# Loading the two norms' scale and offset rows through GpSimd's queue, and making the scaled residual during the down projection

## The chip, the cores and the metric

The kernel runs on one core of one Trainium2 chip. The metric is the device time of one execution in microseconds. The five engines of the core run their own instruction streams and meet at semaphores: TensorE (PE in the rows; PEld is its weight load), VectorE (DVE), ScalarE (ACT), GpSimd (POOL) and SyncE (SP). Transfers are issued by an engine's queue (SPq, ACTq, POOLq in the rows) and carried by 16 DMA engines.

## The reference

One encoder layer on 256 tokens of width 2048. What matters here is its second half: a layer norm, a gated feed-forward of width 5632, a residual, and a second layer norm.

```python
mixed = concat(rms_norm(attn), rms_norm(ssm)) @ w_out
x = layer_norm(ALPHA * x + mixed, ln1_g, ln1_b)          # norm 1
up = x @ w_ffn_in                                         # 2048 -> 2 * 5632
gate = causal_depthwise_conv(up[..., :D_FF], conv_w, conv_b)
hidden = gelu(gate) * up[..., D_FF:]
ff = hidden @ w_ffn_out                                   # 5632 -> 2048
x = layer_norm(ALPHA * x + ff, ln2_g, ln2_b)             # norm 2
```

`ln1_g`, `ln1_b`, `ln2_g` and `ln2_b` are rows of 2048 numbers. The kernel keeps them as four rows of a tensor `rows` in device memory.

## The kernel before

**The stream of weights.** All products take their weights from one stream of chunks of 128x1024 float32 (512 KB). `run` (L176) walks over them. In turn j it splits chunk j+3, issues the load of chunk j+7 on SP's queue, and then writes chunk j's matmuls. A load goes into one of four buffers `raw` (`dma_chunk`, L145). The split (`split_chunk`, L151) makes the high part `hi` on ScalarE (L163) and the rest `lo` on VectorE (L164), each into one of four buffers. So a load waits until VectorE has done with the `raw` buffer four chunks earlier, and a split waits until TensorE has done with the `hi` and `lo` buffers four chunks earlier. SP issues in order: a load behind a waiting one waits too.

**The order.** The code is written out in one order, in which small jobs (`side`) put in a piece after a given chunk; a scheduler then places the instructions on the engines, and each engine runs its own list in order.

**Around norm 1.** The last products of `w_out` (tile `os`) end in `evac_os` (L1112), which adds them onto `res`, the tile [128, 2, 2048] that holds the residual of both token tiles. `ln1` (L1138) normalizes one token tile without scale and offset in place in `res` (L1148; one quarter on ScalarE, L1146), transposes it on TensorE (L1153, tile `lt`), applies scale and offset per partition on ScalarE (L1156, tile `lnt`), and VectorE splits it into the stationary-side activations `x1s` (L1160 and L1161). Norm 1's second token tile runs while TensorE does the first feed-forward product for the first token tile alone (L226).

**Feed-forward.** 44 blocks of four chunks (weights `wf`, tile `f`, `mm_f`, L214) fill the hidden tiles `hid`. Then come 88 chunks of the down projection (weights `wd`, tile `d`, `mm_b`, L237): four column blocks of 22 chunks, each with two PSUM banks, in turns of banks 0, 1 and 2, 3. At a column block's end `evac_down` (L1305) does `res = ALPHA * res + d` on VectorE. `x1s` lies in the buffer tagged `xs`; it is free when the last feed-forward product (chunk 175) has been done.

**The residual.** `res` has to hold norm 1 with its scale and offset before the first `evac_down`. `residual` (L1245) does this in eight pieces of 256 columns: it loads the scale and the offset piece, each broadcast over the partitions, into small tiles `rg` and `rb` (two buffers each) on SP's queue, and GpSimd multiplies and adds them onto both token tiles (L1257, L1258). `load_gb2` (L1266) loads norm 2's two full rows on SP's queue into the buffer `xs`, early in the down projection.

Of the kernel before, what the change touches and what calls it, by code (L numbers as in the profile page):

```python
# [12 lines left out]
F32 = mybir.dt.float32  # L13
# [3 lines left out]
ALU = mybir.AluOpType  # L17
PSUM = bass.MemoryType.PSUM
DRAM = bass.MemoryType.DRAM

P = 128
SEQ = 256
DM = 2048
# [8 lines left out]
NP_ = G // 2  # L32
# [25 lines left out]
def host_layout(x, w_in, attn_rel_bias, ssm_a_re, ssm_a_im, ssm_log_dt, ssm_b_re, ssm_b_im,  # L58
                ssm_c_re, ssm_c_im, ssm_d, w_glu, b_glu, g_attn_out, g_ssm_out, w_out,
                ln1_g, ln1_b, w_ffn_in, ffn_conv_w, ffn_conv_b, w_ffn_out, ln2_g, ln2_b):  # L60
    a = {}
    xs = x[0]
# [21 lines left out]

    # groups by (half, column): pairs as they are, and the order whose transposes are pairs
    col, half = np.arange(NP_)[None, :], np.arange(2)[:, None]
# [32 lines left out]
class Builder:  # L119
# [6 lines left out]

# [1 line left out]
    def fill(self):  # L128
# [8 lines left out]

# [1 line left out]
    def add(self, src, mm, post=None, hold=None):  # L139
# [58 lines left out]

# [1 line left out]
    def mm_a(self, ps, hi, lo, xs, k0, first, last, nk=8):  # L200
# [13 lines left out]
    def mm_f(self, ps, hi, lo, k0, first, last, part=None):  # L214
        """product with x1, whose columns are (token tile, high or low part, token)"""
        nc, xs = self.nc, self.x1
        th = lambda a: a.rearrange("p (t h c) -> p t h c", t=2, h=2)[:, :, 0]
        for kk in range(8):
            x = xs[:, k0 + kk]
            w = slice(kk * P, (kk + 1) * P)  # L220
            start, stop = first and kk == 0, last and kk == 7

            def low():
                nc.tensor.matmul(th(ps), lhsT=lo[:, w], rhs=th(x), start=False, stop=False)  # L224
            if part == 0:
                nc.tensor.matmul(ps[:, 0:SEQ], lhsT=hi[:, w], rhs=x[:, 0:SEQ], start=start, stop=False)  # L226
                continue
            c = slice(0, 512) if part is None else slice(SEQ, 512)
            if stop:
                low()  # L230
            nc.tensor.matmul(ps[:, c], lhsT=hi[:, w], rhs=x[:, c], start=start and part is None, stop=stop)  # L231
            if not stop:
                low()
# [23 lines left out]

# [1 line left out]
    def build(self):  # L259
# [30 lines left out]

    # phase 1 -----------------------------------------------------------------
    def plan_phase1(self):
# [83 lines left out]
        add_v(1)  # L376
        # k, q
        for j in range(8):
            for c in range(4):
# [9 lines left out]
                self.add(I["wkq"][4 * j + c], mm, post)  # L389
        # w_out, attention half  # L390
        def wo_attn(nb, c):
# [8 lines left out]
        for nb in (2, 3):  # L400
            for c in range(4):
                wo_attn(nb, c)
        # glu
        for f in range(8):
# [3 lines left out]
            self.add(I["wg"][f], mm, lambda f=f: self.evac_glu(f, cur["ps"]))  # L408
        # w_out, state half; the last two blocks one token tile after the other
        for nb in range(4):  # L410
# [53 lines left out]
    def evac_ab(self, ps, name, scale=None):  # L464
        """second half of a product of the split operands, copied out of PSUM"""
        t = self.t1([P, SEQ], name)
        if scale is None:
            self.nc.scalar.copy(t, ps[:, SEQ:])
        else:
            self.nc.scalar.mul(t, ps[:, SEQ:], scale)  # L470
        return t
# [34 lines left out]

    # S5 ----------------------------------------------------------------------
    def s5_load(self):
# [40 lines left out]
    def s5_params(self):  # L549
# [46 lines left out]
        exp(dec, dec)  # L596
        # sin and cos by the quadrant of th
        ts(k, th, 0.6366197723675814, MUL, MAGIC, ADD)
# [62 lines left out]
        def cmul(o, ia, a, b, w):  # L661
            # o, a: [P, 2, 4, NP_] tiles at index; (o = a*b)
            (orr, oi), (ar, ai), (br, bi) = o, a, b
# [11 lines left out]
        ts(self.scb[:, 1], self.scb[:, 1], -1.0, MUL)  # L675
        # a^(s) f B, s = 0..3
        MB = self.MB = bp.tile([P, 2, NP_, 4, SG], F32, tag="d0", name="MB")
# [29 lines left out]
        ops.append((0.2, lambda: V.tensor_copy(cB[:, 1], PA[:, 1, 3])))  # L707
        # -C_im
        ts(self.sc[:, 1], self.sc[:, 1], -1.0, MUL)
# [3 lines left out]
    def reorder(self, a, o):  # L713
        """values of the groups in the order of the transposes, brought to the order of the pairs"""
        nc = self.nc
# [112 lines left out]
    def s5_kstack(self):  # L828
# [39 lines left out]
        for g2 in range(2):  # L868
            for i in range(4):
                # rows s >= 3-i hold the kernel of lag s-(3-i)  # L870
                n = SG * (i + 1)
# [5 lines left out]
    def s5_cm(self):  # L877
# [8 lines left out]
        for pg in range(4):  # L886
# [20 lines left out]
            for ri in range(2):  # L907
                # C holds (re, -im): re(C a) and -im(C a)
                Gp.tensor_tensor(t0, cr if ri == 0 else ci, ar, op=ALU.mult)
# [42 lines left out]
    def evac_glu(self, f, ps):  # L952
# [7 lines left out]
        nc.vector.tensor_tensor(s, ps[:, 0:SEQ], t, op=ALU.add)  # L960
        # sigmoid(z) = (1 + tanh(z / 2)) / 2; the half is taken at the group's norm
        nc.scalar.activation(s, s, AF.Tanh, bias=self.bh[:, f:f + 1], scale=0.5)
# [35 lines left out]

    # attention -----------------------------------------------------------------
    def attention(self, j):  # L1000
# [85 lines left out]

    # w_out and layer norm 1 ------------------------------------------------------
    def load_x(self):
# [81 lines left out]

    # phase 2 -----------------------------------------------------------------
    def plan_phase2(self):
# [37 lines left out]
        for nb in range(4):  # L1210
            for c in range(22):
# [29 lines left out]
                self.add(I["wd"][22 * nb + c], mm, post if c == 21 else None, hold)  # L1241
        self.side(12, self.residual())
        self.side(178, self.load_gb2())

    def residual(self):  # L1245
        nc, fp = self.nc, self.fp
        for q in range(8):
            c = slice(q * 256, (q + 1) * 256)
            g = fp.tile([P, 256], F32, tag="rg", name=f"rg{q}")
            b = fp.tile([P, 256], F32, tag="rb", name=f"rb{q}")  # L1250
            nc.sync.dma_start(g, self.I["rows"][0, c].partition_broadcast(P))
            nc.sync.dma_start(b, self.I["rows"][1, c].partition_broadcast(P))
            yield
            yield
            for tt in range(2):
                r = self.res[:, tt, c]
                nc.gpsimd.tensor_tensor(r, r, g, op=ALU.mult)  # L1257
                nc.gpsimd.tensor_tensor(r, r, b, op=ALU.add)  # L1258
            yield

# [4 lines left out]

    def load_gb2(self):  # L1266
        nc = self.nc
        t = self.bp.tile([P, 2, DM], F32, tag="xs", name="gb2")
        self.g2, self.b2 = t[:, 0], t[:, 1]
        nc.sync.dma_start(self.g2, self.I["rows"][2].partition_broadcast(P))  # L1270
        nc.sync.dma_start(self.b2, self.I["rows"][3].partition_broadcast(P))
        self.st2 = [self.cp.tile([P, n, 6], F32, name=f"st2{n}") for n in (4, 8)]
        yield
# [75 lines left out]
```

## Time and profile before

| | before |
|---|---|
| median of 3 runs | 1163.69 us (1162.95 to 1164.85) |
| span of the profiled execution, first to last instruction | 1161.2 us |
| median of the runs less that span | 2.5 us |
| TensorE busy | 1120.5 us, 96% of the span |
| VectorE / ScalarE / GpSimd busy | 67% / 48% / 10% |
| mean granted TensorE clock | 0.985 |

The profile is of one execution. Its spans, waits and clocks are read in microseconds from the first instruction. [...]

### The profile page before, as it was taken

Reading aid. Unit: us, or ns where it says so; the run is one execution under the profiler, and the core shown is the slowest. Engines: PE = TensorE matmul, PEld = TensorE weight load, DVE = VectorE, ACT = ScalarE, POOL = GpSimd, SP = SyncE. Lnnn points to the kernel's source line nnn. Section 1 sums busy time; section 2 is a strip of 40 time slices with the busy share of each in tenths; the row PEclk is TensorE's granted clock in tenths of the full one; section 3 lists DMA queues with packets and bytes.
Section 4 is the critical chain, followed back from the end, with each engine's and each line's share of the span. In section 5 each row is a group of like instructions: output and inputs, shape, how many; then the busy total and the mean of one; then the engine's idle time right before and its main releaser. Section 6 shows DMA issues by size and latency. Waiting matters only on the chain.

```text
span 1161.2 us, 18034 instructions
## 1 busy us (share of the span) xinstructions
PE 1120.5 (96%) x6936; PEld 946.9 (82%) x6936; DVE 772.8 (67%) x1379; ACT 563.1 (48%) x849; POOL 121.6 (10%) x125
## 2 busy tenths in 40 slices
PE   8999959999999889999999999999999999999996
PEld 6887747887787778888888888888888888888885
DVE  7993399994678866666666666666666545454555
ACT  5454325553666545555555555555555433333350
POOL 2031870000001270000000000000000000000001
PEclk9999979999999989999999999999999999999998
DMA  8786324443666446556656666666665766666661
GB/s 299 281 234 147 104 83 146 155 150 97 225 193 204 150 140 212 183 182 189 190 184 183 194 185 182 185 187 190 185 186 190 258 196 192 193 196 192 190 198 73
DMA packets 63589, 212.04 MB, mean 183 GB/s; under 512 B 7568, under 2 KB 13072, under 8 KB 62864
## 3 DMA queue, kind: packets, MB, share of 16 engines
q1 hardware_dynamic: 62320, 208.38, 57.7%
q0 software_dynamic: 896, 2.10, 0.8%
q8 instruction: 54, 0.88, 0.3%
q10 hardware_dynamic: 288, 0.43, 0.1%
q14 instruction: 31, 0.25, 0.1%
HBM read 207.46 MB, written 3.41 MB: 182 GB/s over the span
## 4 chain that ended last, share of the span: by engine, by line
PE 88%; DVE 7%; DMA 2%; POOL 1%; issue 1%; ACT 1%; SPq 0%; ACTq 0%; POOLq 0%; DVEq 0%
PE f L231 27%; PE f L224 14%; PE d L247 7%; PE d L249 7%; PE d L245 7%; PE kq L209 3%; PE u L209 2%; DVE lo L164 2%; PE kq L211 2%; PE oa L245 1%; PE oa L247 1%; PE u L211 1%; PE oa L249 1%; PE glu L209 1%; PE v L247 1%; PE v L249 1%
## 5 line engine op out<-in xcount | busy, mean ns | idle before, releaser
L164 DVE TENSOR_TENSOR lo<-raw,hi 128x1024 fp32r<-128x1024 f32 (+1 forms) x358 | 441.0, 1233 | 246.0 <-ACT hi L163 242.2
L163 ACT CAST hi<-raw 128x1024 fp32r<-128x1024 f32 (+1 forms) x358 | 374.4, 1046 | 299.8 <-PE d L249 125.9
L231 PE MATMUL f<-x1s,hi 128*128 128x512 f32 (+1 forms) x1408 | 491.2, 398 | 6.4 <-ACT hi L163 4.2
L224 PE MATMUL f<-x1s,lo 128*128 128x256 f32 x1408 | 382.6, 283 | 0.5 <-DVE lo L164 0.5
L231 PEld LDWEIGHTS f<-x1s,hi 128*128 128x128 f32 x1408 | 261.2, 190 | 63.1 <-ACT hi L163 4.5
L224 PEld LDWEIGHTS f<-x1s,lo 128*128 128x128 f32 x1408 | 268.0, 190 | 9.5 <-DVE lo L164 1.0
L247 PE MATMUL d<-lo,hid 128*128 128x512 f32 (+1 forms) x360 | 133.4, 371 | 0.0
L245 PE MATMUL d<-hi,hid 128*128 128x512 f32 (+1 forms) x360 | 133.4, 370 | 0.0
L249 PE MATMUL d<-hi,hid 128*128 128x512 f32 (+1 forms) x360 | 133.3, 370 | 0.0
L209 PE MATMUL kq<-xs,hi 128*128 128x512 f32 x240 | 89.8, 412 | 3.1 <-DVE qt L505 3.1
L1324 POOL TENSOR_TENSOR res<-res,gb 128x416 f32<-128x416 f32 x2 | 2.9, 1444 | 721.6 <-ACT res L1323 721.6
L245 PEld LDWEIGHTS d<-hi,hid 128*128 128x128 f32 x360 | 67.8, 188 | 11.8
L247 PEld LDWEIGHTS d<-lo,hid 128*128 128x128 f32 x360 | 67.8, 188 | 11.6
L249 PEld LDWEIGHTS d<-hi,hid 128*128 128x128 f32 x360 | 67.8, 188 | 11.5
L211 PE MATMUL kq<-xs,lo 128*128 128x256 f32 x240 | 69.2, 288 | 0.0
L209 PEld LDWEIGHTS kq<-xs,hi 128*128 128x128 f32 x240 | 45.6, 190 | 14.5 <-DVE qt L505 3.5
L1279 ACT COPY ga<-f 128x256 f32<-128x256 f32 x44 | 16.4, 374 | 82.4 <-PE f L231 82.4
L1286 DVE TENSOR_TENSOR gp<-f,ga 128x256 f32<-128x256 f32 x44 | 18.7, 425 | 45.0 <-ACT ga L1279 45.0
L1279 ACT COPY va<-f 128x256 f32<-128x256 f32 x44 | 16.3, 371 | 64.7 <-PE f L231 64.7
L1298 DVE TENSOR_TENSOR va<-f,va 128x256 f32<-128x256 f32 x44 | 18.7, 424 | 42.3 <-ACT va L1279 42.3
L211 PEld LDWEIGHTS kq<-xs,lo 128*128 128x128 f32 x240 | 45.8, 191 | 0.9
L209 PE MATMUL u<-xs,hi 128*128 128x512 f32 x120 | 43.5, 401 | 0.0
(214 smaller groups left out, 1418.1 us busy)
## 6 DMA issues: line engine op xcount, KB each, us to landing
raw<-wf SPq DMA_DIRECT2D x176, 512.0 KB, 3.7
raw<-wd SPq DMA_DIRECT2D x88, 512.0 KB, 4.3
raw<-wkq SPq DMA_DIRECT2D x32, 512.0 KB, 3.6
raw<-wo SPq DMA_DIRECT2D x32, 512.0 KB, 3.9
raw<-wu SPq DMA_DIRECT2D x16, 512.0 KB, 4.5
raw<-wv SPq DMA_DIRECT2D x15, 512.0 KB, 6.1
raw<-wg SPq DMA_DIRECT2D x8, 512.0 KB, 4.4
bd<-band SPq DMA_DIRECT2D x16, 128.0 KB, 3.0
```

The source lines that it names most:

```text
L163: self.nc.scalar.copy(hi[:, c], raw[:, c])
L164: self.nc.vector.tensor_tensor(lo[:, c], raw[:, c], hi[:, c].bitcast(F32), op=ALU.subtract)
L209: nc.tensor.matmul(ps, start=first and kk == 0, stop=False, **h)
L211: nc.tensor.matmul(ps[:, 0:SEQ], start=False, stop=False, **l)
L224: nc.tensor.matmul(th(ps), lhsT=lo[:, w], rhs=th(x), start=False, stop=False)
L231: nc.tensor.matmul(ps[:, c], lhsT=hi[:, w], rhs=x[:, c], start=start and part is None, stop=stop)
L245: nc.tensor.matmul(ps, lhsT=ah, rhs=wh, start=first and kk == 0, stop=False)
L247: nc.tensor.matmul(ps, lhsT=ah, rhs=wl, start=False, stop=False)
L249: nc.tensor.matmul(ps, lhsT=al, rhs=wh, start=False, stop=last and kk == 1)
L1279: self.nc.scalar.copy(tv, v[:, :, 1])
L1286: nc.vector.tensor_tensor(g[:, 2:].rearrange("p (t c) -> p t c", t=2), p0, t, op=ALU.add)
L1298: nc.vector.tensor_tensor(tv, p0, tv, op=ALU.add)
```

## The change

`residual` and `load_gb2` are gone. In their place one job `load_gb` is put in after chunk 176, the first chunk of the down projection. It loads all four rows in full, each 2048 columns broadcast over 128 partitions (1 MB written each), by GpSimd's queue into one tile of the buffer `xs`. Behind them on GpSimd stand the multiplications and additions of the residual, now in four column blocks of 512. Norm 2 reads its rows from the same tile. The rest of the difference is comments.

```diff
-        self.side(12, self.residual())
-        self.side(178, self.load_gb2())
-
-    def residual(self):
-        nc, fp = self.nc, self.fp
-        for q in range(8):
-            c = slice(q * 256, (q + 1) * 256)
-            g = fp.tile([P, 256], F32, tag="rg", name=f"rg{q}")
-            b = fp.tile([P, 256], F32, tag="rb", name=f"rb{q}")
-            nc.sync.dma_start(g, self.I["rows"][0, c].partition_broadcast(P))
-            nc.sync.dma_start(b, self.I["rows"][1, c].partition_broadcast(P))
-            yield
-            yield
-            for tt in range(2):
-                r = self.res[:, tt, c]
-                nc.gpsimd.tensor_tensor(r, r, g, op=ALU.mult)
-                nc.gpsimd.tensor_tensor(r, r, b, op=ALU.add)
-            yield
+        self.side(176, self.load_gb())
...
-    def load_gb2(self):
+    def load_gb(self):
+
         nc = self.nc
-        t = self.bp.tile([P, 2, DM], F32, tag="xs", name="gb2")
-        self.g2, self.b2 = t[:, 0], t[:, 1]
-        nc.sync.dma_start(self.g2, self.I["rows"][2].partition_broadcast(P))
-        nc.sync.dma_start(self.b2, self.I["rows"][3].partition_broadcast(P))
+        t = self.bp.tile([P, 4, DM], F32, tag="xs", name="gb")
+        self.g2, self.b2 = t[:, 2], t[:, 3]
+        for i in range(4):
+            nc.gpsimd.dma_start(t[:, i], self.I["rows"][i].partition_broadcast(P))
+        for nb in range(4):
+            c = slice(nb * 512, (nb + 1) * 512)
+            for tt in range(2):
+                r = self.res[:, tt, c]
+                nc.gpsimd.tensor_tensor(r, r, t[:, 0, c], op=ALU.mult)
+                nc.gpsimd.tensor_tensor(r, r, t[:, 1, c], op=ALU.add)
```

On SP's queue, at the head of the feed-forward, this is the list before and after (`raw` are the weight buffers; `raw_4488` is the eighth feed-forward chunk, chunk 7, `raw_4510` chunk 8; minus marks what is only in the kernel before):

```order
 L148 DMA raw_4488<-wf 128x1024
-L1251 DMA rg_4995<-rows 128x256
-L1252 DMA rb_4996<-rows 128x256
-L1251 DMA rg_5085<-rows 128x256
-L1252 DMA rb_5086<-rows 128x256
...
-L1251 DMA rg_5432<-rows 128x256
-L1252 DMA rb_5433<-rows 128x256
 L148 DMA raw_4510<-wf 128x1024
```

Twelve loads of `rg` and `rb` stood between the loads of chunk 7 and chunk 8; now chunk 8's load is next behind chunk 7's. (Four more stood further ahead, between two loads of `wo`.)

On GpSimd the list between the small memsets `gp` at the head of the feed-forward and the end of the program is now this:

```order
68 L1186 MEMSET gp_4366 128x2
69 L1186 MEMSET gp_4367 128x2
70 L1255 DMA gb<-rows 128x2048 x4
71 L1260 TENSOR_TENSOR res<-res,gb 128x512 x2
72 L1261 TENSOR_TENSOR res<-res,gb 128x512 x2
...
79 L1314 TENSOR_TENSOR res<-res,gb 128x416
```

The 32 operations on 256 columns behind the memsets are gone; 16 operations on 512 columns stand behind four loads, and in front of norm 2's own pieces.

Early in the down projection SP's queue held this in the kernel before (`raw_9148` is the last load ahead of norm 2's rows):

```order
347 L148 DMA raw_9148<-wd 128x1024
348 L1270 DMA gb_9229<-rows 128x2048
349 L148 DMA raw_9177<-wd 128x1024
350 L148 DMA raw_9197<-wd 128x1024
351 L1271 DMA gb_9229<-rows 128x2048
352 L148 DMA raw_9215<-wd 128x1024
```

Both `gb` loads have left this queue, which holds only weight loads there now. The lists of TensorE, VectorE and ScalarE have the same operations in the same order as before.

## Rows read from the trace of the kernel before

**Rows 1.** The page: span, busy time, a queue (packets, MB, share), issues (us to landing).

```profile
span 1161.2 us, 18034 instructions
PE 1120.5 (96%) x6936; PEld 946.9 (82%) x6936; DVE 772.8 (67%) x1379; ACT 563.1 (48%) x849; POOL 121.6 (10%) x125
...
q0 software_dynamic: 896, 2.10, 0.8%
...
gb<-rows SPq DMA_DIRECT2D x2, 1024.0 KB, 7.1
...
udr<-ut POOLq DMA_DIRECT2D x8, 128.0 KB, 4.7
```

**Rows 2.** Stretches: length, busy by engine (instructions), granted clock, DMA share, GB/s.

```profile
400.00:410.00 10.00, 6.93 (x45) 6.40 (x44) 8.05 (x13) 7.01 (x19) 7.25 (x9) 0.83 0.22 62
...
430.00:440.00 10.00, 8.92 (x34) 7.32 (x35) 8.46 (x12) 6.70 (x12) 0.00 (x0) 0.66 0.77 251
...
910.00:920.00 10.00, 10.00 (x46) 8.29 (x45) 5.49 (x6) 4.00 (x6) 0.00 (x0) 1.00 0.99 351
```

**Rows 3.** The chain that ended last, 419 to 432: start, length, what.

```profile
419.38 2.91 DMA rb<-rows
...
423.71 5.71 DMA raw<-wf
429.52 1.05 ACT hi L163
430.60 1.24 DVE lo L164
```

**Rows 4.** TensorE's timeline, 420 to 440: start, length, instruction, [idle before <-releaser].

```profile
420.41 0.63 PE L231 MATMUL f<-x1s,hi 128*128 128x512 f32 x2
...
426.05 0.40 PE L231 MATMUL f<-x1s,hi 128*128 128x512 f32 x1
430.62 0.79 PE L231 MATMUL f<-x1s,hi 128*128 128x512 f32 x1 [4.17 <-ACT hi L163]
...
439.42 0.63 PE L231 MATMUL f<-x1s,hi 128*128 128x512 f32 x2
```

**Rows 5.** SP's issues, 375 to 440.

```profile
375.55 18.48 SPq L148 DMA_DIRECT2D raw<-wf  x8
...
423.71 15.77 SPq L148 DMA_DIRECT2D raw<-wf  x9
```

**Rows 6.** Timeline around norm 1's second token tile: TensorE, GpSimd and VectorE.

```profile
401.50 2.02 PE L1153 MATMUL lt<-ident,res 128*128 128x128 f32 x16 [0.85 <-issue]
405.73 0.39 PE L231 MATMUL f<-x1s,hi 128*128 128x256 f32 x1 [2.21 <-DVE x1s L1161]
...
389.95 2.61 POOL L1258 TENSOR_TENSOR res<-res,rb 128x256 f32<-128x256 f32 x2
...
395.17 0.67 DVE L1161 TENSOR_TENSOR x1s<-lnt,x1s 128x512 fp32r<-128x512 f32 x1
...
404.58 1.09 DVE L1161 TENSOR_TENSOR x1s<-lnt,x1s 128x512 fp32r<-128x512 f32 x1
...
411.14 1.76 DVE L164 TENSOR_TENSOR lo<-raw,hi 128x1024 fp32r<-128x1024 f32 x1
```

**Rows 7.** Weight loads between 895 and 950: landing times.

```profile
DMA to landing us min/median/max: 3.6/4.3/6.5
```

**Rows 8.** Down projection, timeline: SP's issues, ScalarE and VectorE.

```profile
908.97 0.33 SPq L1270 DMA_DIRECT2D gb<-rows  x1
...
914.46 1.05 ACT L163 CAST hi<-raw 128x1024 fp32r<-128x1024 f32 x1 [1.67 <-PE d L249]
...
915.55 1.23 DVE L164 TENSOR_TENSOR lo<-raw,hi 128x1024 fp32r<-128x1024 f32 x1 [1.50 <-ACT hi L163]
...
968.33 1.28 DVE L1309 SCALAR_TENSOR_TENSOR res<-res,d 128x512 f32<-128x512 f32 x2
```

**Rows 9.** A GpSimd group of the first phase: count, busy us, mean ns of one.

```profile
L909 POOL TENSOR_TENSOR kcm<-prm 128x512 f32<-128x512 f32 x8 | 11.1, 1388 | 0.7
```

## The prediction

> **What bounds the kernel now.** I read the page first, then the chain that ended last, then TensorE's and SP's timelines at the two places that the change touches. The profiled execution spans 1161.2 us [rows 1]; the median of the runs is 2.5 us above that span, and I add this to every result, so that sums are made in the span and compared with 1163.7. TensorE is busy in 96% of it [rows 1] and the chain runs through its products nearly everywhere. A change off TensorE is therefore worth only what TensorE waits for it, or loses in clock behind such a wait.
>
> The chain has one place where it leaves TensorE for the work that this change removes. From 419 to 429 us it runs through a load of `rb`, then through a load of weights that takes 5.71 us, then through ScalarE's and VectorE's split of it, and only then back to TensorE [rows 3]. SP's timeline says why the weights are late: eight loads of `wf` go out in 18.48 us from 375.55, and the next one only at 423.71 [rows 5]. Between them stand the twelve loads of `rg` and `rb` that the change shows there. Each waits for a small buffer, that is, for GpSimd, which is busy in 7.25 of the 10 us from 400 [rows 2]. The weights' load behind them, of feed-forward chunk 8, was ready to go when VectorE had split chunk 4: that split ends at 411.14 + 1.76 = 412.9 [rows 6]. So it went out 10.8 us late. Chunks 4 to 7 were in hand, and TensorE ate them up: its last product is at 426.05, the next at 430.62 after 4.17 us of waiting for `hi` [rows 4].
>
> A smaller loss lies just ahead, around norm 1's second token tile. TensorE sits idle 0.85 us ahead of the transposes and 2.21 us ahead of the first product that needs `x1s` [rows 6], and from 400 to 410 its granted clock is 0.83 [rows 2]. GpSimd's residual operations run beside VectorE there, and VectorE's operations are longer beside them: the same L1161 takes 0.67 us at 395.17 and 1.09 us at 404.58, and the split L164 1.76 us at 411.14 where it takes 1.23 us in the down projection [rows 6, 8].
>
> **What is removed, term one: the stalled weight load.** Two feed-forward chunks take 426.05 - 420.41 = 5.64 us between equal places. From 426.05 the next such place should have come at 431.69; it came at 439.42 [rows 4]. The loss is 7.7 us. Of this 4.17 us is the wait; the rest is mostly clock: from 430 to 440 the granted clock is 0.66 [rows 2]. [...] What could be late next without the small loads? With chunk 8's load sent at 412.9, taking as long as the late one (5.71 us), and the split's 1.05 and 1.24 us behind it [rows 3], chunk 8 is ready by about 421.2, against 426.3 where TensorE wants it. Nothing is left of the stall: I take the whole 7.7 us.
>
> **Term two: norm 1 without GpSimd beside it.** The upper bound is all of the idle time and clock there: 0.85 + 2.21 + 1.7, the last from a clock of 0.83 over 10 us (3.4 us at the lower level) [rows 2, 6]; 4.8 us. The lower bound is nothing, if ScalarE rather than VectorE sets the pace. I take the following. The 0.85 us goes: the two additions of offsets at 389.95 run for 2.61 us [rows 6] beside VectorE's work ahead of the statistics, and a handful of operations, each 0.4 to 0.5 us shorter, give more than 0.85. Of the 2.21 us, about 0.9 goes: the cast and the subtraction that make the first quarter of `x1s` lose about 0.4 us each, as L1161 does, and the rest is ScalarE's scale and offset, which stays. Of the clock's 1.7 I take a third, 0.55, since the shorter wait may or may not lower the clock, and the last quarter of `x1s` comes hardly sooner. That is 2.3 us.
>
> **What is added in the down projection.** Four loads of 1 MB, 4.19 MB in all, now leave from GpSimd's queue when `x1s` is free; before, two of them left from SP's queue at 908.97 and 914.46 [rows 8]. They land between the weights' loads, and the question is whether those come late. One chunk takes 1.05 + 1.67 = 2.72 us there (split, and wait for the buffer) [rows 8], so the weights need 512 KB in 2.72 us, 193 GB/s. The spare time of a load: VectorE gives the buffer back at 915.55 + 1.23 = 916.8, ScalarE wants it filled four chunks after 914.46, at 925.3; that is 8.5 us, of which a landing takes 4.3 [rows 7], so 4.2 us to spare. The split starts three chunks ahead of its use, 8.2 us, and takes 2.3 us, so there are 5.9 us more: about 10 us in all before TensorE waits. From 910 to 920 the engines are 99% busy and move 351 GB/s [rows 2]. If all four loads went ahead of every weight, they would take 4.19 MB at 351 GB/s, 11.9 us, and TensorE would wait 1.9 us. If they go behind, nothing. The nearest row is the kernel before: half of these bytes stood ahead of the weights in their own queue, the worst landing was 6.5 us [rows 7], and ScalarE went on waiting for TensorE and not for a load [rows 8]. I take nothing, and keep 1.9 us for the range.
>
> [...] No row here shows two busy queues side by side.
>
> GpSimd's 16 operations of 512 columns take 1.39 us each with little beside them [rows 9] and 2.6 us with VectorE beside them (two of 256 columns took 2.61) [rows 6]: 22 to 42 us. They start when two rows have landed, at the latest about 921, and end by 963 at the latest. `evac_down` needs the first four of them at 968.33 [rows 8] and the other column blocks 22 chunks, 60 us, apart. So VectorE does not wait. VectorE's split, 1.23 us, grows to 1.76 us beside them, covered by the 1.50 us that it idles ahead of each [rows 8]; without that cover it would cost 0.5 us a chunk. TensorE's, ScalarE's and VectorE's lists keep their order, so nothing else moves.
>
> **The sum.** 7.7 + 2.3 = 10.0 us off: a span of 1151.2, and 1163.7 - 10.0 = **1153.7 us**.
>
> **Rivals.**
> *Only the stall goes.* ScalarE's chain sets the pace in norm 1: 1163.7 - 7.7 = 1156.0. For it: ScalarE was busy 7 of the 10 us from 400 [rows 2]. Against it: the 2.21 us wait ends with VectorE [rows 6].
> *Another wait takes the stall's place.* The head of the feed-forward finds another late buffer or load and TensorE stalls there anyway; with term two alone, at best 1161.4, otherwise about 1163.7. Against it: chunk 8 has 5 us to spare by the rows above.
> *The four rows hold the engines.* GpSimd's queue moved 2.10 MB in 0.8% of 16 engines' span, 9.3 us of all of them [rows 1]. At that pace 4.19 MB take 18.6 us; with the weights wholly behind, TensorE waits 8.6 us and loses 3.4 us of clock as at 430: 1165.7, 0.17% above before. With part of it, 1155 to 1160.
> *VectorE stands behind the residual (the other side).* If GpSimd's queue brings large rows at the pace of its small ones, 128 KB in 4.7 us [rows 1], 28 GB/s, the first two rows need 75 us and land at 984; with four operations the first block is ready at 990 and `evac_down` at 968.3 waits 21 us, with the splits queued behind it on VectorE. TensorE has 5.9 us to spare, then waits 15 us and loses 3.4 us of clock: 1172. This decides the sign once the block is ready 12.5 us after `evac_down` wants it, near 981. Against it: on SP's queue 1 MB landed in 7.1 us [rows 1], so a small load's time is mostly fixed.
>
> **How the numbers follow.** Chances: my forecast 0.72, only the stall 0.13, another wait 0.06, engines held 0.06, VectorE behind the residual 0.03. A measurement of this kernel can tell about 0.2%, 2.3 us, from no change. Faster by more: the first two, two thirds of the engines held, a third of another wait, 0.91. Within 0.2%: what is left of these two, 0.06. Slower: 0.03. The range: at the low end all of term two's bound, 7.7 + 4.8 = 12.5 us off, 1151.2; at the high end only the stall and most of the rows' 1.9 us lost, 1157.5. This holds the first two cases but for their edges, a little over 8 in 10.
>
> **What would show it.** On SP, weight loads without a gap near 412. No wait of TensorE near 424, and a clock of 1.00 in the stretch that was 0.66. VectorE's L1161 at 0.67 us in norm 1's second half, no 0.85 us ahead of the transposes. In the down projection `gb` landing within 20 us, weights' landings at most 14 us, ScalarE still waiting for TensorE. The forecast is wrong if ScalarE waits for `raw` after 909, or VectorE for `res` at the first `evac_down`.

## The result, and the profile of the changed kernel

| | before | after |
|---|---|---|
| median of 4 runs each, side by side | 1164.27 us (1162.95 to 1165.29) | 1152.03 us (1150.71 to 1152.71) |
| ratio, 95% interval | | 0.9895 (0.9883 to 0.9907) |
| span of the profiled execution | 1161.2 us | 1150.3 us |

The changed kernel is 12.2 us faster by the medians and 10.9 us by the two profiled spans; the prediction was 1153.7 us, with 10.0 us off, in a range of 1151.2 to 1157.5. The other 1.3 us are not in the two profiles: where a single run has its time and its own span on record, the time is 1.7 to 2.2 us above the span, in both kernels. By that the profiled execution of the kernel before was about 1 us quicker than the median one, and the 2.5 us that the prediction added to its spans hold this difference too.

The page of the changed kernel. TensorE's busy time fell by 4.9 us only; the rest of the 10.9 us was idle time [rows 1].

```profile
span 1150.3 us, 17982 instructions
...
PE 1115.6 (97%) x6936; PEld 944.2 (82%) x6936; DVE 775.0 (67%) x1379; ACT 563.4 (49%) x849; POOL 123.3 (11%) x113
```

The same stretches as in [rows 2], and one more, of the changed kernel.

```profile
400.00:410.00 10.00, 8.46 (x72) 8.23 (x72) 6.55 (x12) 7.46 (x20) 0.00 (x0) 1.00 0.00 0
430.00:440.00 10.00, 10.00 (x59) 8.68 (x58) 6.97 (x9) 4.84 (x8) 0.00 (x0) 1.00 0.69 198
910.00:920.00 10.00, 10.00 (x46) 8.29 (x45) 3.92 (x2) 2.83 (x3) 9.95 (x7) 1.00 0.90 351
920.00:930.00 10.00, 10.00 (x45) 8.28 (x45) 9.63 (x5) 5.61 (x6) 10.00 (x6) 1.00 0.60 162
```

Both places that had lost clock are at 1.00 now: 400 to 410 (0.83 before) and 430 to 440 (0.66 before). TensorE's timeline shows the idle times (start, length, instruction, [idle before]).

```profile
400.54 1.91 PE L1153 MATMUL lt<-ident,res 128*128 128x128 f32 x16
...
403.99 0.39 PE L231 MATMUL f<-x1s,hi 128*128 128x256 f32 x1 [1.53 <-DVE x1s L1161]
...
417.19 0.63 PE L231 MATMUL f<-x1s,hi 128*128 128x512 f32 x2
...
422.82 0.63 PE L231 MATMUL f<-x1s,hi 128*128 128x512 f32 x2
...
428.39 0.62 PE L231 MATMUL f<-x1s,hi 128*128 128x512 f32 x2
```

The 0.85 us ahead of the transposes are gone, the wait for `x1s` is 1.53 us instead of 2.21 [rows 6], and the three instructions that repeat 5.6 us apart pass the old stall without a wait. Where the kernel before stood at 420.41 the changed one stands at 417.19, and where it stood at 439.42 the changed one stands at 428.39 [rows 4]: 3.2 us came from norm 1, and 11.0 - 3.2 = 7.8 us from the stall. At the first `evac_down` (968.33 before [rows 8], 957.40 now) the distance is 10.9 us still, so nothing was given back in between. The first phase ran 0.5 us later in this execution, as VectorE's first L1148 shows, so norm 1 itself gained 3.7 us (before, then after):

```profile
387.08 2.33 DVE L1148 TENSOR_SCALAR res<-res,mv 128x512 f32<-128x512 f32 x4
```

```profile
387.57 1.91 DVE L1148 TENSOR_SCALAR res<-res,mv 128x512 f32<-128x512 f32 x4
...
402.78 0.43 DVE L1160 CAST x1s<-lnt 128x512 fp32r<-128x512 f32 x1 [1.94 <-ACT lnt L1156]
403.24 0.69 DVE L1161 TENSOR_TENSOR x1s<-lnt,x1s 128x512 fp32r<-128x512 f32 x1
```

From this first L1148 to the first `evac_down` it is 581.2 us before and 569.8 us after, 11.4 us less. The first L1148 lies anywhere from 385.9 to 388.2 us in the profiles of this document, so where two profiles are compared below, this distance is the safer measure.

SP's issues have no gap any more (375 to 440, against 423.71 in [rows 5]):

```profile
376.04 63.84 SPq L148 DMA_DIRECT2D raw<-wf  x21
```

In the down projection, GpSimd's and VectorE's timelines, then, from two views, what ScalarE waited for from 880 to the end, and how long the weights' loads from 884 to 939 took:

```profile
898.31 2.23 POOL L1255 DMA_DIRECT2D gb<-rows  x4 [531.61 <-PE f L231]
906.37 3.53 POOL L1260 TENSOR_TENSOR res<-res,gb 128x512 f32<-128x512 f32 x2 [5.84 <-DMA gb<-rows]
...
931.95 4.51 POOL L1261 TENSOR_TENSOR res<-res,gb 128x512 f32<-128x512 f32 x2
```

```profile
901.90 1.23 DVE L164 TENSOR_TENSOR lo<-raw,hi 128x1024 fp32r<-128x1024 f32 x1 [0.94 <-ACT hi L163]
...
920.37 3.76 DVE L164 TENSOR_TENSOR lo<-raw,hi 128x1024 fp32r<-128x1024 f32 x2 [3.21 <-ACT hi L163]
921.81 2.32 DVE L164 TENSOR_TENSOR lo<-raw,hi 128x1024 fp32r<-128x1024 f32 x1
...
957.40 1.28 DVE L1299 SCALAR_TENSOR_TENSOR res<-res,d 128x512 f32<-128x512 f32 x2
```

```profile
ACT hi L163 <- PE d L249: 110.5, 67, 1.8
...
ACT hi L163 <- DMA raw<-wd: 17.4, 11, 4.0
```

```profile
DMA to landing us min/median/max: 3.5/4.6/13.3
```

The weights did come late here: a load took up to 13.3 us (6.5 before [rows 7]), and ScalarE waited 11 times for one, 17.4 us in all. Still TensorE ran without a wait, at a clock of 1.00 (from 900 to 930). How close that was can be worked out. VectorE's splits are due every 2.72 us from 901.90 on, so the sixth one should end at 901.90 + 5 x 2.72 + 1.23 = 916.7; it began at 920.37 and ended near 921.9, as the next one began (the line at 920.37 holds both, the line at 921.81 the second alone). That is 5.2 us late, the most of any split there, and the prediction had found 5.9 us that TensorE can bear.

### The profile page after: what moved, and what is told of

It reads as the page before. It is cut to its first block, busy times and chain, and to the rows that moved or that the text cites. A ratio compares the mean times of both kernels' runs of the same rounds, so it can differ in the third digit from the quotient of the medians.

```text
span 1150.3 us, 17982 instructions
## 1 busy us (share of the span) xinstructions
PE 1115.6 (97%) x6936; PEld 944.2 (82%) x6936; DVE 775.0 (67%) x1379; ACT 563.4 (49%) x849; POOL 123.3 (11%) x113
## 4 chain that ended last, share of the span: by engine, by line
PE 91%; DVE 6%; ACT 1%; issue 1%; DMA 1%; SPq 0%; POOL 0%; ACTq 0%; POOLq 0%
PE f L231 28%; PE f L224 15%; PE d L247 7%; PE d L249 7%; PE d L245 7%; PE kq L209 4%; PE u L209 2%; PE kq L211 2%; DVE lo L164 2%; PE oa L245 1%; PE oa L247 1%; PE u L211 1%; PE oa L249 1%; PE glu L209 1%; PE os L249 1%; PE v L247 1%
## 5 line engine op out<-in xcount | busy, mean ns | idle before, releaser
L164 DVE TENSOR_TENSOR lo<-raw,hi 128x1024 fp32r<-128x1024 f32 (+1 forms) x358 | 448.0, 1254 | 230.0 <-ACT hi L163 226.0
L231 PE MATMUL f<-x1s,hi 128*128 128x512 f32 (+1 forms) x1408 | 487.2, 396 | 1.5 <-DVE x1s L1161 1.5
L231 PEld LDWEIGHTS f<-x1s,hi 128*128 128x128 f32 x1408 | 258.7, 188 | 57.6 <-DVE x1s L1161 1.8
```

The source lines that it names most:

```text
L164: self.nc.vector.tensor_tensor(lo[:, c], raw[:, c], hi[:, c].bitcast(F32), op=ALU.subtract)
```

## The experiments

Twelve kernels ran, in four groups. The kernel before ran beside each group, with medians of 1163.2, 1162.8, 1163.6 and 1163.5 us.

| run | us, median (range) | ratio to before, 95% interval |
|---|---|---|
| small loads and residual taken out | 1151.74 (1151.44 to 1151.87) | 0.9898 (0.9885 to 0.9912) |
| before with six small buffers | 1160.73 (1159.23 to 1161.07) | 0.9974 (0.9964 to 0.9985) |
| changed, GpSimd beside norm 1 | 1159.95 (1158.15 to 1160.64) | 0.9967 (0.9955 to 0.998) |
| changed, rows on SP's queue | 1151.67 (1151.07 to 1151.81) | 0.9897 (0.9884 to 0.9911) |
| changed, more bytes | 1152.47 (1151.41 to 1152.73) | 0.9908 (0.9895 to 0.9922) |
| changed, GpSimd behind norm 1 | 1152.51 (1152.3 to 1153.83) | 0.9913 (0.9899 to 0.9926) |
| changed, rows in two pairs | 1151.78 (1151.13 to 1152.67) | 0.9902 (0.9887 to 0.9917) |
| changed, loads one by one | 1155.23 (1153.11 to 1157.24) | 0.9934 (0.9921 to 0.9947) |
| changed, late load, seven pieces | 1153.59 (1152.84 to 1154.03) | 0.9912 (0.9898 to 0.9925) |
| changed, late load, eight pieces | 1155.18 (1153.16 to 1158.14) | 0.9939 (0.9925 to 0.9952) |
| changed, late load, five pieces on res | 1153.59 (1153.0 to 1154.79) | 0.9915 (0.9902 to 0.9928) |
| changed, late load, six pieces on res | 1158.49 (1154.62 to 1159.96) | 0.9952 (0.9937 to 0.9967) |

**Does what is added cost anything?** The kernel before, without the residual's loads and operations:

```diff
-        self.side(12, self.residual())
```

> The kernel before without the residual's scale and offset (this part of the computation is left out); norm 2's two rows are still loaded by SP's queue. Theory A, what the change adds costs nothing: as fast as the changed kernel, 1152.0 us, ratio 0.9895. Theory B, the four loads or GpSimd's work in the down projection hide a loss inside the changed kernel: 1 to 4 us faster than it, 1148 to 1151 us. TensorE's wait of 4.17 us near 430 is gone in both.

1151.74 us and a span of 1150.1, against 1152.03 and 1150.3 for the changed kernel. The removal alone makes the whole gain, and the four rows and 16 operations in the down projection cost nothing that can be measured: from the first L1148 to the first `evac_down` it is 569.8 us in both.

**The stall alone taken away.** The kernel before, with more small buffers, so that SP's loads need not wait for GpSimd:

```diff
-            g = fp.tile([P, 256], F32, tag="rg", name=f"rg{q}")
-            b = fp.tile([P, 256], F32, tag="rb", name=f"rb{q}")
+            g = fp.tile([P, 256], F32, tag="rg", bufs=6, name=f"rg{q}")
+            b = fp.tile([P, 256], F32, tag="rb", bufs=6, name=f"rb{q}")
```

> The kernel before with six buffers each for rg and rb in place of two: the same loads on SP and the same operations on GpSimd, but only the last four loads wait for GpSimd. Theory A, the small buffers' wait on SP's queue is what stalled the weights, worth 7.7 us by itself: 1156.6 us (1155.5 to 1158), no wait of TensorE for hi near 430, and norm 1 as slow as before, with a wait for x1s of 2 us or more and a granted clock below 1.00 there. Theory B, GpSimd's operations beside VectorE and ScalarE make the stall too, not the loads: 1162 us or more, the stall is still there.

Only some 3 us of the 7.7 came (0.26% by the ratio, 2.5 us by the medians), which neither theory had forecast. The stall is gone, but norm 1 became slower. GpSimd's timeline, two windows, and TensorE's waits from 380 to 450 (us in total, times, longest):

```profile
387.57 1.80 POOL L1257 TENSOR_TENSOR res<-res,rg 128x256 f32<-128x256 f32 x2 [20.81 <-PE lt L1153]
...
398.33 2.03 POOL L1258 TENSOR_TENSOR res<-res,rb 128x256 f32<-128x256 f32 x2
```

```profile
390.00:400.00 10.00, 7.49 (x59) 7.01 (x58) 10.00 (x11) 3.46 (x10) 10.00 (x10) 1.00 0.36 107
400.00:410.00 10.00, 7.55 (x48) 7.11 (x49) 7.81 (x17) 5.45 (x15) 4.94 (x7) 0.83 0.10 28
```

```profile
PE f L231 <- DVE x1s L1161: 3.2, 4, 2.1
PE f L226 <- DVE x1s L1161: 2.9, 3, 2.2
```

GpSimd now worked without a pause until 400.4, beside norm 1's first token tile, and VectorE was busy all of 390 to 400. In the kernel before GpSimd stood still from 392.6 to 402.0: its two buffers held pieces whose second half had to wait for the transposes of norm 1's second tile (GpSimd's timeline before):

```profile
401.99 1.59 POOL L1257 TENSOR_TENSOR res<-res,rg 128x256 f32<-128x256 f32 x2 [9.43 <-PE lt L1153]
```

The same shortage of buffers that starved the weights kept GpSimd out of norm 1's way. From the first L1148 to the first `evac_down` it is 577.9 us here, 8.0 us above the changed kernel with no stall in it.

**GpSimd beside norm 1, without the loads.** The changed kernel, with 32 operations on `res` that change nothing (times 1, plus 0):

```diff
+        self.side(12, self.idle_ops())
...
+                nc.gpsimd.tensor_tensor(r, r, one, op=ALU.mult)
+                nc.gpsimd.tensor_tensor(r, r, zero, op=ALU.add)
```

> The changed kernel with 32 GpSimd operations on res at the old place, times one and plus zero, from tiles that need no load. Theory A, GpSimd beside VectorE in norm 1 costs the other 3.7 us by itself: 1155.7 us (1154 to 1157), the waits of 0.85 and about 2.2 us are back, the granted clock from 400 to 410 falls below 1.00, and there is no stall near 430. Theory B, that part came from the loads or from SP: 1152.0 us, norm 1 as in the changed kernel.

1159.95 us, 7.9 above the changed kernel, with no stall near 430. Two windows, TensorE's waits, and VectorE's timeline of this run:

```profile
400.00:410.00 10.00, 6.79 (x40) 6.05 (x40) 8.08 (x17) 3.94 (x11) 8.39 (x11) 0.83 0.01 2
410.00:420.00 10.00, 9.16 (x62) 8.84 (x63) 9.28 (x10) 5.86 (x14) 10.00 (x11) 0.83 0.07 8
```

```profile
PE f L226 <- DVE x1s L1161: 2.5, 2, 2.2
PE f L231 <- DVE x1s L1161: 2.4, 2, 2.2
```

```profile
394.70 1.24 DVE L1161 TENSOR_TENSOR x1s<-lnt,x1s 128x512 fp32r<-128x512 f32 x1
395.86 0.96 DVE L1160 CAST x1s<-lnt 128x512 fp32r<-128x512 f32 x1
396.74 0.74 DVE L1118 SCALAR_TENSOR_TENSOR res<-os,rs,res 128x512 f32<-128x512 f32 x1
...
405.80 1.45 DVE L1148 TENSOR_SCALAR res<-res,mv 128x512 f32<-128x512 f32 x3
```

The second tile's L1148 starts at 405.80, at 399.38 in the changed kernel. From the first L1148 to the first `evac_down` it is 577.8 us, 7.9 us above the changed kernel and as with six buffers. So GpSimd costs far more beside norm 1 than the 3.7 us of the kernel before, if nothing holds it back; both this run and the one with six buffers missed what my two terms, taken one by one, had led me to expect.

**The same operations behind norm 1.** The run above, with a first operation on GpSimd that reads the last quarter of `x1s`:

```diff
+        nc.gpsimd.tensor_scalar(one.rearrange("p (k t) -> p k t", t=P), self.x1[:, 14:16, SEQ + P:2 * SEQ].bitcast(F32), 0.0, 1.0, op0=ALU.mult, op1=ALU.add)
```

> The kernel of the run with 32 GpSimd operations in norm 1, with one change: a GpSimd operation ahead of them reads the last quarter of x1s (times 0, plus 1), so that they start only when VectorE has finished norm 1, near 405 us. My theory: GpSimd costs time only beside norm 1, where VectorE is what TensorE waits for; later VectorE has time to spare: 1152.0 us (1151.3 to 1152.8), no wait of TensorE for x1s longer than in the changed kernel, full clock from 400 to 420. The rival: 32 operations beside VectorE at the head of the feed-forward cost wherever they stand, because the splits grow from 1.23 to 1.76 us or more: 1155 to 1160, with TensorE waiting for lo.

1152.51 us: the same 32 operations cost 0.5 us, which these runs cannot tell from nothing; from the first L1148 to the first `evac_down` it is 569.8 us, as in the changed kernel. VectorE is 94% busy and its splits grow to 1.76 us, but TensorE's only wait is the changed kernel's own, and its clock is 1.00 (a window, TensorE's waits, VectorE's timeline):

```profile
410.00:420.00 10.00, 10.00 (x64) 8.94 (x64) 9.37 (x10) 7.90 (x12) 10.00 (x9) 1.00 0.62 206
```

```profile
PE f L231 <- DVE x1s L1161: 1.5, 1, 1.5
```

```profile
413.17 1.76 DVE L164 TENSOR_TENSOR lo<-raw,hi 128x1024 fp32r<-128x1024 f32 x1
```

**The late load, with GpSimd kept off norm 1's first tile.** A first attempt put five loads, one after the other through one buffer, on SP's queue; GpSimd only copies one column each time.

```diff
+        self.side(12, self.one_by_one(), 2000)
...
+            nc.sync.dma_start(g, self.I["rows"][q % 4, 0:1536].partition_broadcast(P))
+            nc.gpsimd.tensor_copy(s[:, q:q + 1], g[:, 0:1])
```

> The changed kernel with five unused loads of 128x1536 put into one buffer on SP's queue, four of them between the weight loads of chunks 7 and 8; GpSimd does only five operations on one column that free the buffer. This makes the stall of the kernel before without GpSimd beside VectorE. My theory: four loads of about 6.5 us one after the other from 396 hold chunk 8's load until about 422; TensorE then waits about 3 us near 424 to 429 and loses 2 to 3.5 us of clock behind that: 1157 to 1160 us, with norm 1 as quick as in the changed kernel (second tile's L1148 at 399 to 400 us, full clock from 400 to 410). The rival: the loss near 430 in the kernel before came with GpSimd's work and the lowered clock of norm 1, and a late load alone costs no more than its wait: 1154 to 1156.

It tells nothing of the stall. A step took 4.2 us and not 6.5, and chunk 8's load left at 410.4, in time. The 3 us that the run lost come from elsewhere: its priority changed the order on VectorE and ScalarE, and TensorE waited 2.8 us at 460 for VectorE's `va`, the value half of the gated product. In all other runs these two engines keep the changed kernel's order.

Two further kernels kept the other engines' lists and put back the small loads, two buffers each, with GpSimd working on a scratch tile and started late by a load of its own. They have 7 and 8 pieces:

```diff
+        self.side(12, self.pieces())
...
+            nc.gpsimd.dma_start(w, self.I["rows"][q, 0:1536].partition_broadcast(P))
...
+            nc.sync.dma_start(g, self.I["rows"][0, c].partition_broadcast(P))
+            nc.sync.dma_start(b, self.I["rows"][1, c].partition_broadcast(P))
+            nc.gpsimd.tensor_tensor(s, g, b, op=ALU.mult)
+            nc.gpsimd.tensor_tensor(s, s, b, op=ALU.add)
```

> The changed kernel with seven pieces of rg and rb on SP's queue again (two buffers each), used by GpSimd on a scratch tile only (14 operations on 256 columns, res untouched), and started behind a load of 128x1536 on GpSimd's queue that itself waits for norm 1's first tile. Ten of the small loads stand between the weight loads of chunks 7 and 8, and the other engines' lists are as in the changed kernel. So GpSimd is kept off norm 1 until about 404 us, and the stall is there alone. My theory: chunk 8's load leaves near 419.5 and not at 409; TensorE wants it at 422.9, 6.4 us after a load can leave in time (landing 4.2, split 2.3), so it waits about 3 us and loses up to 3.4 us of clock behind that: 1156 to 1159 us. The rival, that the loss near 430 came from GpSimd and the clock of norm 1, and that a late load alone costs no more than its wait: 1153.5 to 1155.5.

> The same with eight pieces, so that one more small load holds the weights on SP, by about 3 us, and chunk 8's load leaves near 422.5. My theory: a wait of TensorE of about 6 us and 3.4 us of clock: 1159 to 1162 us, 3 us above the run with seven pieces. The rival (only the wait): 1157 to 1158.5.

GpSimd's operations took about 0.75 us on their own, less than I had reckoned, so the loads left sooner than planned and both times came out below the forecast. They also began sooner, at 400.7 and 399.7 and not near 404, so they run beside norm 1's second tile. With seven pieces SP sends chunk 8 at 414.41 and TensorE does not wait for it; its 1.6 us above the changed kernel go with norm 1, where the profiled execution has a wait of 1.9 us for `x1s` and a clock of 0.83 from 400 to 410; its time lies in the rival's range, but without a wait for the load it does not test the rival. With eight it leaves at 415.82 (SP's timeline), and TensorE waits for it, for 1.1 us (TensorE's timeline):

```profile
415.82 28.23 SPq L148 DMA_DIRECT2D raw<-wf  x14
```

```profile
422.86 0.49 PE L231 MATMUL f<-x1s,hi 128*128 128x512 f32 x1 [0.35 <-ACT hi L163]
...
424.12 0.39 PE L224 MATMUL f<-x1s,lo 128*128 128x256 f32 x1 [0.77 <-DVE lo L164]
```

The last pair has four operations for each piece, as the kernel before, that read `res` and write a scratch tile, behind norm 1's first quarter of the second tile (in the traces four of them run ahead of it, from 400.0 and 398.6); 5 and 6 pieces:

```diff
+        nc.gpsimd.tensor_copy(s[:, 0, 0:1], self.x1[:,3,SEQ+P:SEQ+P+1].bitcast(F32))
...
+            for tt in range(2):
+                nc.gpsimd.tensor_tensor(s[:, tt], self.res[:, tt, c], g, op=ALU.mult)
+                nc.gpsimd.tensor_tensor(s[:, tt], s[:, tt], b, op=ALU.add)
```

> The changed kernel with five pieces of rg and rb on SP's queue again (two buffers each, six small loads between the weight loads of chunks 7 and 8). For each, GpSimd does four operations on 256 columns, as in the kernel before, into a scratch tile (res untouched), and it starts when VectorE has made the first quarter of x1s for norm 1's second tile, near 404 us, so that only the rest of norm 1 has GpSimd beside it. Piece 4's loads wait for piece 2's operations, three pieces of 3.5 to 5 us from 404: chunk 8's load leaves near 416 to 418. In the earlier run with 415.8 TensorE waited 1.1 us. My theory (from about 414.7 on, each us that the load leaves later is one of TensorE's waiting, and a wait of some us brings a clock loss of up to 3.4 us): a wait of 1.5 to 3.5 us, 1154 to 1158 us. The rival, that the loss near 430 of the kernel before came from GpSimd's operations and not from the load: GpSimd runs there in this kernel too, so 1157 or more without any wait for hi.

> The same with six pieces, eight small loads between chunks 7 and 8: the weight load has to wait for one piece more, 4 to 5 us, and leaves near 420 to 423. My theory: TensorE waits 5.5 to 8 us for hi near 424 and its clock is lowered behind that, 1160 to 1163 us, 4 to 6 us above the run with five pieces, though norm 1 and GpSimd's work up to there are the same. The rival: one piece more of GpSimd's work, behind norm 1, costs nothing, as in the run with 32 operations there: the same time as with five pieces within 1 us.

Norm 1 is the same in both (waits for `x1s` of 2.0 and 0.46 us), and one piece more on SP's queue makes 4.9 us. With five pieces chunk 8's load leaves at 414.72 and TensorE does not wait for it. With six (SP's timeline, TensorE's timeline, and a window):

```profile
418.34 26.19 SPq L148 DMA_DIRECT2D raw<-wf  x13
```

```profile
422.59 0.40 PE L224 MATMUL f<-x1s,lo 128*128 128x256 f32 x2
...
425.05 0.50 PE L231 MATMUL f<-x1s,hi 128*128 128x512 f32 x1 [1.83 <-ACT hi L163]
...
426.31 0.38 PE L224 MATMUL f<-x1s,lo 128*128 128x256 f32 x1 [0.76 <-DVE lo L164]
...
432.88 0.40 PE L224 MATMUL f<-x1s,lo 128*128 128x256 f32 x2
```

```profile
420.00:430.00 10.00, 7.41 (x32) 5.91 (x31) 4.93 (x7) 5.09 (x9) 3.71 (x6) 0.83 0.80 272
```

From 422.59 the next equal place is 10.29 us away instead of 5.64: 4.65 us lost, 2.6 of it waiting; the rest is mostly clock, by an estimate 1.7 us (0.17 of the 10 us that read 0.83). From the first L1148 to the first `evac_down` the two runs differ by as much, 575.9 against 571.3 us. Both forecasts lay a little too high, again because the load left sooner. The rival, that GpSimd's operations and not the load made the loss, is out: a piece behind norm 1 costs nothing by the run with 32 of them.

Together with the kernel before this gives a row of doses. "First use" is TensorE's first product with chunk 8.

| kernel | load leaves | behind the first L1148 | first use | TensorE's waits for `hi` and `lo` | lowest clock of the 10-us windows behind it |
|---|---|---|---|---|---|
| seven pieces | 414.41 | 27.4 us | no wait | 0 | 1.00 |
| five pieces on res | 414.72 | 27.1 us | no wait | 0 | 1.00 |
| eight pieces | 415.82 | 29.9 us | 422.86 | 1.1 us | 1.00 |
| six pieces on res | 418.34 | 32.2 us | 425.05 | 2.6 us | 0.83 |
| before | 423.71 | 36.6 us | 430.62 | 4.6 us | 0.66 |

In the three with a wait, the first use comes 7.0, 6.7 and 6.9 us behind the load's issue. Each row is one profiled execution; the one with eight pieces was the fastest of its five (1153.2 us, the median is 1155.2), so its clock of 1.00 need not be that of the others. The table holds for a norm 1 about as quick as in the changed kernel: with six buffers and with GpSimd beside norm 1 the load left 30 us behind the first L1148 too, and TensorE, held up in norm 1, came late enough not to wait for it.

**What stands behind the rows in the down projection.** The four rows on SP's queue (and two chunks later):

```diff
-        self.side(176, self.load_gb())
+        self.side(178, self.load_gb())
...
-            nc.gpsimd.dma_start(t[:, i], self.I["rows"][i].partition_broadcast(P))
+            nc.sync.dma_start(t[:, i], self.I["rows"][i].partition_broadcast(P))
```

> The changed kernel with the four full rows loaded by SP's queue, two chunks later, where norm 2's rows were loaded before. Theory A, only the bytes count and the spare time of about 10 us takes them: 1152.0 us, within 1 us of the changed kernel. Theory B, the second queue matters, since in one queue each weight load behind a row waits for the whole row: the weights come up to 11.9 us late, TensorE waits about 2 us near 920 and may lose clock behind it, 1154 to 1157 us.

Two of the rows on GpSimd's queue ahead of the residual's operations, and two behind:

```diff
-        for i in range(4):
+        for i in range(2):
             nc.gpsimd.dma_start(t[:, i], self.I["rows"][i].partition_broadcast(P))
...
+        for i in range(2, 4):
+            nc.gpsimd.dma_start(t[:, i], self.I["rows"][i].partition_broadcast(P))
```

> The changed kernel, with norm 2's two rows loaded behind the residual's operations on GpSimd, so that 2.1 MB and not 4.2 stand beside the weights at first. My theory: the weights' landings near 900 to 940 fall from at most 13.3 us to under 10, ScalarE waits less for them, and the time stays at 1152.0 within 0.7, since TensorE waited for nothing there. The rival: late weights cost something that the trace doesn't show; then the time falls to 1151.2 or lower.

And 1.57 MB more among the rows:

```diff
+        nc.gpsimd.memset(t[:, 0, 0:1], 0.0)
+        for i in range(2):
+            x = self.fp.tile([P, 1536], F32, tag=f"more{i}", bufs=1, name=f"more{i}")
+            nc.gpsimd.tensor_copy(x[:, 0:1], t[:, 0, 0:1])
+            nc.gpsimd.dma_start(x, self.I["rows"][i, 0:1536].partition_broadcast(P))
```

> The changed kernel with two more loads of 128x1536 (1.57 MB, unused) among the four rows on GpSimd's queue. My theory: in the changed kernel the weights beside the rows use up nearly all the time that TensorE has to spare near 920 us (VectorE's split about 5.2 us behind its schedule, 5.9 us to spare), so 1.57 MB more, 4 us of all engines at the 388 GB/s that 900 to 910 shows, bring TensorE to wait 1 to 3 us there and lower its clock behind that: 1153.5 to 1157 us. The rival: the lateness is set by GpSimd beside VectorE and not by bytes; then TensorE waits for nothing and the time stays at 1152.0.

All three are at 1151.7 to 1152.5 us, like the changed kernel. From the first L1148 to the first `evac_down` it is 569.8, 569.8 and 570.0 us. What differs is the weights' lateness. With the rows in two pairs ScalarE waited 6.6 us for `raw` in all, and the slowest weights took 9.2 us from 884 to 939. With the rows on SP's queue (ScalarE's waits for `raw`, and the weights' landings in the same stretch):

```profile
ACT hi L163 <- DMA raw<-wd: 3.7, 2, 2.7
```

```profile
DMA to landing us min/median/max: 3.4/4.1/8.6
```

With more bytes my theory of 1 to 3 us of waiting fell: the splits came at most 5.9 us late (the eighth ended at 927.1 and was due at 901.00 + 7 x 2.72 + 1.23 = 921.3), 0.7 us later than in the changed kernel and not 4. The rows then land later, and GpSimd starts at 920.0 instead of 906.4, so VectorE's splits are not yet lengthened while the weights are late. The edge shows nevertheless, and only just (waits of TensorE's weight loads, 890 to 960):

```profile
PEld d L247 <- DVE lo L164: 0.3, 1, 0.3
```

None of the other runs shows a wait of TensorE for a split in this stretch; this one has 5.9 us of lateness, as much as the spare time worked out, and the split that was waited for is that eighth one.

## Why the prediction was right, by its own steps

**Term one, 7.7 us, was right in size and cause.** The trace gives 7.8 us, and the doses above show the cause by itself: one load of weights, held back on SP, makes TensorE wait from a departure between 27 and 30 us behind the first L1148 on (norm 1 being quick), and the longer waits went with lower clocks (1.1, 2.6 and 4.6 us with 1.00, 0.83 and 0.66). The 3.4 us of clock in the prediction's sums is an estimate, 0.34 of the 10 us that read 0.66 [rows 2]; 7.7 - 4.17 = 3.5 us were lost besides the wait. The lower level that it names is in none of its rows. The trace of the kernel before shows it: in stretches of 1 us the clock is 0.50 from 431 to 436 and 1.00 from 437 on, with an L231 of 128x512 every 0.64 us in the first and every 0.36 us in the second, and it is 0.50 from 407 to 409 too. The prediction took 8.3 us from a load's departure to its use, up to the end of the split on VectorE (412.9 to 421.2; its own three terms add up to 8.0); 6.7 to 7.0 us were measured, since TensorE begins with `hi`, which ScalarE makes first.

**Term two was mis-sized: 2.3 us forecast, 3.7 us measured.** The 0.85 us went as forecast, and of the 2.21 us 0.68 instead of 0.9. The step that failed is "of the clock's 1.7 I take a third": the clock was 1.00 from 400 to 410, so all 1.7 us, an estimate from the 0.83, came back. These make 3.2 us. Another 0.4 us came from norm 1's first tile, which the prediction left out: its transposes on TensorE ran from 387.68 to 390.12, 2.44 us, before, and take 2.02 us now (TensorE's timeline, before, then after):

```profile
387.68 1.57 PE L1153 MATMUL lt<-ident,res 128*128 128x128 f32 x12
389.46 0.66 PE L1153 MATMUL lt<-ident,res 128*128 128x128 f32 x4 [0.21 <-DVE res L1148]
```

```profile
388.17 2.02 PE L1153 MATMUL lt<-ident,res 128*128 128x128 f32 x16
```

VectorE's four L1148 ahead of them took 2.33 us beside GpSimd and take 1.91 us alone. The share of VectorE's pace was read rightly: in the changed kernel VectorE stands 1.94 us until ScalarE's `lnt` comes, and the cast and the subtraction behind it, 0.43 and 0.69 us, are most of the 1.53 us that TensorE still waits.

**The two terms are not independent, and the prediction treated them so.** With buffers enough to end the stall, GpSimd's work moves further into norm 1 and costs 8.0 us there and not 3.7, so only about 3 of the 7.7 us are gained. The sum held because the change takes both away; that either term can be had by itself was not shown, and for the stall it was not so.

**Additions at nothing: right, with less to spare than claimed.** The bound of 10 us before TensorE waits was made of 4.2 us at the buffer and 5.9 at the split; the splits used 5.2 of the 5.9. VectorE's split grew to 2.32 us, not 1.76. It stayed below the 2.72 us between chunks, so VectorE caught up: ahead of the split at 939.94 it was idle for 1.26 us again. GpSimd ended at 936.5, by 963 at the latest as forecast, and `evac_down` found its block ready.

The prediction named ScalarE's waiting for `raw` after 909 as a sign that it was wrong. It happened, and the time did not suffer: the sign was badly chosen, since behind such a wait the split still has 5.9 us before TensorE wants it. The rows' last landing took 19.0 us and the slowest weights 13.3 us; the prediction's limits for them, 20 and 14 us, were its author's estimates, as none of its rows shows two busy queues side by side. The weights fell 9.0 us behind (13.3 against the median of 4.3 before [rows 7]): of the 10 us to spare, about 1 was left. From 900 to 910, with a load of weights under way from 900.65 on, both queues moved at once, and the weights got 0.86 of 3.88 MB, 22%. What set that share is not shown.

**Rivals.** Only the stall goes: out, by norm 1's 3.7 us. Another wait in the stall's place and VectorE behind the residual do not appear in the trace. The rows did hold the weights, but by less than TensorE can bear (5.2 of 5.9 us). The median of 1152.03 lies 0.8 us above the low end of the range: term two gave 1.4 us more than was taken, and the medians differ by 0.8 us more than the 11.4 us of the two profiles, which no step of the prediction covers; as four runs of one kernel spread by 2 us, it may be chance.

## What to carry to other kernels

A load behind small loads that wait for a slow engine is late by that engine's time, and by what that engine waits for itself (here the transposes of norm 1's second tile, 9.43 us); look in the issuing queue's timeline for a gap ahead of the transfer that the critical engine ends up waiting for. When such a stall is taken away by more buffers, ask what the stall had held back: here it was GpSimd, which then took 8.0 us of norm 1 instead of 3.7, most of what was won. Work for an engine that slows another belongs where the slowed one has time to spare (behind norm 1, or in the down projection); there it cost 0.5 and 0.3 us by the medians, which these runs cannot tell from nothing.

## What the runs showed of the hardware

GpSimd beside VectorE lengthens some of VectorE's operations and not others. Subtractions with both inputs in SBUF go from 0.69 to 1.24 us (128x512), and from 1.23 to 1.76 us beside GpSimd's operations on 256 columns and to 2.32 us beside those on 512 (128x1024). The cast of 128x512, which has one input only, goes from 0.43 to 0.96 us. L1118, which has one of its inputs in PSUM, stays as it was (0.74 and 0.75). GpSimd's own operation on 128x512 goes from 1.29 to 2.27 us. Why some lengthen and others do not is not shown.

The same four rows of 1 MB land in 8.0 to 19.0 us on GpSimd's queue beside the weights, and in 5.3 to 9.6 us on SP's, between them; the weights' slowest landing is 13.3 us in the first case and 8.6 in the second.

A wait of TensorE of 1.5 to 2 us went with a clock of 1.00 in some profiled executions (1.53 us at 403.99 in the changed kernel; 2.0 us in the run with five pieces on res) and with 0.83 in another (1.9 us, seven pieces). Some runs with waits of that size spread widely, 1153.2 to 1158.1 us with eight pieces and 1154.6 to 1160.0 with six on res, and others do not, 1153.0 to 1154.8 with five on res; where the residual is left out it is 1151.4 to 1151.9. That the spread is the clock's is not shown, as each kernel has one profile.
